# Opening of an encoder kernel: a broadcast weight row, small gate weights, the third unit's weights and the decay sums take other places

## The chip, the cores and the metric

The kernel runs on one core of one Trainium2 chip, as one launch. The metric is the device time of one execution in microseconds (us). Before the change it is 1990.61 us, the median of 3 runs (1989.9 to 1991.65). One further execution was profiled; the profile and its trace are of that one.

The engines are named as the profile names them: PE multiplies matrices (PEld is the loading of its stationary operand), DVE and ACT work on vectors, POOL is the general-purpose engine, SP issues the DMAs. Each engine takes its instructions strictly in the order in which they stand in its own queue. Matrix products go to PSUM, in banks of 128 x 512 numbers; the other tiles lie in SBUF.

## The reference

One layer of an encoder: 1024 tokens and 16 meta tokens of width 1024. The input is normalised, multiplied by one wide matrix `w_in`, and cut into the inputs of two mixers; what matters here is the first one and, in it, the small gates.

```python
h = rmsnorm(h_res, norm1_w[l])
proj = h @ w_in[l]
(q, k, v, z, b_raw, a_raw, sc_b, sc_c, sc_x, gate_a, gate_b) = jnp.split(proj, SPLIT_POINTS, axis=-1)
o_dn = gated_deltanet_bidir(q, k, v, z, b_raw, a_raw, ...)
...
qkv = jax.nn.silu(depthwise_conv_centred(jnp.concatenate([q, k, v], axis=-1), conv_w))
beta = jax.nn.sigmoid(b_raw).reshape(Bsz, L, 2, DN_HEADS)
g = -jnp.exp(A_log) * jax.nn.softplus(a_raw.reshape(Bsz, L, 2, DN_HEADS) + dt_bias)
...
g = jnp.cumsum(g, axis=-1)      # in each chunk of 64 tokens, forwards and backwards
decay = jnp.exp(jnp.where(tri, g[..., :, None] - g[..., None, :], -jnp.inf))
```

The decay `g` is one number for each token, head (8) and direction (2). Its running sums set the decay factors of the scan over chunks that follows. The scan's outputs, a second mixer (a short convolution), a merge, an output projection and a gated feed-forward block make up the rest of the layer.

## The kernel before

Every product of two float32 matrices is made of three PE passes: each operand is split into a high part (the number cast to the type in which PE works, on ACT) and a low part (the difference, on DVE or POOL), and high x high, low x high and high x low are added in one PSUM bank (`dense_steps`, line 331). The normalised, transposed input lies in SBUF as 8 high tiles and 8 low tiles (`hTh`, `al`).

The projection is made of **units** of 128 columns of `w_in`. A unit's weights are fetched by a DMA into one of two raw buffers (`pick`, line 932), split into `wh` and `wl` in four parts (`split_part`, lines 939 and 942: two casts on ACT, two subtractions on DVE), and then 72 matmuls run over the tokens in three chunks. A chunk's bank is copied out by two ACT instructions (lines 387 and 388) when the unit's generator is taken one step past the chunk's last matmul. There are two slots of `wh` and `wl`, and the raw buffer of a unit is free for the next DMA when its low part is made.

The first phase is a hand-ordered **opening** and then a **planned** loop. In the opening nine token tiles of x are loaded (`load`, lines 1008 to 1011), and go through `root` (mean square on ACT, two small POOL instructions for the reciprocal root), `scaled` (one DVE instruction at line 1020 that multiplies a tile by its root and by the row `w1row`, the 1024 norm weights laid on all 128 partitions), `turned` (eight PE transposes, line 83), `highs` (line 1039, ACT) and `lows` (line 1045, DVE). Between them run the first two units (`gen0`, the keys of head 0, and `gen1`, its queries; `steps` takes eight steps, which is one chunk) and the small gates: `small_gates` multiplies the 32 gate columns, whose high and low parts stand in one tile `wba` of 64 columns, with the tokens of a chunk (lines 1051 and 1052). The low half of `wba` is made by DVE at line 1118. `keep_warm` is idle PE work.

After the opening a planner writes the instructions of all engines in one order. It keeps its own clocks `T` of the engines; PE's matmuls are the frame, and jobs (convolutions, gates, decays, inverses, scans) put a piece in when the planner's clock says that its inputs are there. `g_gates` (from line 1192) is the job that turns the small gates into `g` and its sums: transposes of `baT` (line 1205), a chain of small DVE instructions for the logarithm (lines 1212 to 1246), an `affine_select` on POOL that clears the unused rows of the last chunk (line 1250), two copies into the tiles `gc` by direction (line 1255), and for each direction four matmuls with triangular matrices (line 1261) and one more (line 1273). The jobs' pieces stand in the same queues as everything else, so a PE instruction that waits for one of them holds up the units' matmuls behind it.

The lines behind the opening that matter: lines 1298 to 1303 take `gen0` and `gen1` to their ends (which writes the copies of their last chunks), queue `g_gates`, and pick the next two units; the third unit (the values of head 0) is split at the loop's start.

Of the kernel before, what the change touches and what calls it, by code (L numbers as in the profile page):

```python
# [8 lines left out]
F32 = mybir.dt.float32  # L9
# [3 lines left out]
ALU = mybir.AluOpType  # L13
# [3 lines left out]
P = 128  # L17
D = 1024
KT = 8
SEQ = 1024  # L20
META = 16
# [16 lines left out]
def encoder_layer(ctx: ExitStack, tc: tile.TileContext, x, meta, norm1_w, w_in,  # L38
                  dn_conv_w, A_log, dt_bias, dn_norm_w, sc_conv_w, w_bdn, w_bsc,
                  w_out, norm2_w, w_gu, w_down, final_w, out):  # L40
    nc = tc.nc
    x, out = x[0], out[0]
# [22 lines left out]
    def psd():  # L65
        return ps.tile([P, 512], F32, tag="e", name=uid("pe"), bufs=2)
# [29 lines left out]
    def wtiles(shape):  # L96
        return [wp.tile(shape, F32R, tag=g, name=uid(g), bufs=2) for g in ("wh", "wl")]
# [104 lines left out]
    c1 = ph1.enter_context(tc.tile_pool(name="c1", bufs=1))  # L202
# [15 lines left out]
    def on(e, ns, ready=0.0):  # L218

        T[e] = max(T[e], ready, T["pe"]) + ns  # L220
        return T[e] + TOPE
# [766 lines left out]
    with tc.tile_pool(name="st", bufs=1) as st:  # L988
# [17 lines left out]
        def load(t):  # L1006
            if t == 0:
                nc.sync.dma_start(xs[0][:META], meta)
                nc.sync.dma_start(xs[0][META:P], x[0:P - META])
            else:  # L1010
                nc.sync.dma_start(xs[t][:size(t)], x[P * t - META:P * t - META + size(t)])
# [6 lines left out]
        def scaled(t):  # L1018
            p = size(t)
            nc.vector.scalar_tensor_tensor(out=xs[t][:p], in0=xs[t][:p], scalar=rss[t][:p, 1:2], in1=w1row[:p],  # L1020
                                           op0=ALU.mult, op1=ALU.mult)
# [35 lines left out]
        def steps(g, n=KT):  # L1057
            for _ in range(n):
                next(g)
# [5 lines left out]
                transpose(idle[:, :P], ident)  # L1065

        load(0)
        load(1)
        nc.sync.dma_start(w1row, norm1_w[0:1, :].broadcast_to([P, D]))
        load(2)  # L1070
        u0 = pick()
        load(3)
# [41 lines left out]
        nc.scalar.copy(cols[:, :24], pt2[:, :24])  # L1114
        nc.scalar.mul(cols[:, 24:25], pt2[:, 24:25], 0.5)
        nc.scalar.copy(wba[:, :, 0:32], raw_ba)
        scaled(3)
        nc.vector.tensor_tensor(out=wba[:, :, 32:64], in0=raw_ba, in1=wba[:, :, 0:32].bitcast(F32), op=ALU.subtract)
        nc.scalar.copy(u1[1][0], u1[2])
        nc.gpsimd.tensor_tensor(out=u1[1][1], in0=u1[2], in1=u1[1][0].bitcast(F32), op=ALU.subtract)  # L1120
        root(4)
# [36 lines left out]
        lows(8, 0)  # L1158
        lows(8, 1)
        steps(gen0)  # L1160
        steps(gen1)
        small_gates(2)


# [27 lines left out]
    def g_gates():  # L1192
# [4 lines left out]
        nc.sync.dma_start(dtb, dt_bias.rearrange("a b c -> a (b c)").broadcast_to([P, 16]))  # L1197
        nc.sync.dma_start(alg, A_log.rearrange("a b c -> a (b c)").broadcast_to([P, 16]))
        nc.gpsimd.memset(BA, 0.0)
        pba = psd()  # L1200
        pbm = psd()
        for c in range(9):
# [33 lines left out]
        for k in (13, 11, 9, 7, 5, 3, 1):  # L1236
# [6 lines left out]
        nc.vector.tensor_scalar(out=alg, in0=alg, scalar1=-1.0, scalar2=None, op0=ALU.mult)  # L1243
        g = sr
        nc.vector.scalar_tensor_tensor(out=g, in0=a_, scalar=0.0, in1=sr, op0=ALU.max, op1=ALU.add)
        nc.vector.tensor_tensor(out=g, in0=g, in1=alg.unsqueeze(1).broadcast_to([P, 9, 16]), op=ALU.mult)
        nc.vector.tensor_scalar(out=beta, in0=beta, scalar1=0.5, scalar2=0.5, op0=ALU.mult, op1=ALU.add)
        on("dve", 1200)

        nc.gpsimd.affine_select(out=g[:, 8, :], in_=g[:, 8, :], compare_op=ALU.is_gt, fill=0.0,  # L1250
                                base=META, pattern=[[0, 16]], channel_multiplier=-1)
        gcs = [c1.tile([P, 8, 9], F32, name=f"gc{d}") for d in range(2)]
        yield T["dve"] + 700
        for d in range(2):
            nc.vector.tensor_copy(gcs[d].rearrange("p h c -> p c h"), g[:, :, d * 8:d * 8 + 8])
            small_v()
        yield T["dve"] + TOPE
        for d in range(2):
            pt = psd().rearrange("p (a n) -> p a n", a=4)
            for i, m in enumerate((U2[d], U[d], E_[d], ones)):  # L1260
# [34 lines left out]
    for m_ in meta_inv:  # L1295
        nc.gpsimd.memset(m_, 0.0)
    SPL = (4, 6, 8, 10)
    for g in (gen0, gen1):
        for _ in g:
            pass  # L1300
    decs.append([g_gates(), T["pe"], None])
    ahead = [pick(), pick()]
    ahead[0][1] = wtiles([P, KT, P])
    while done < H or qkv_units or fill_units or any(ahead):
        u = ahead.pop(0)
        if u is None:
# [558 lines left out]
```

## Time and profile before

| what | value |
|---|---|
| median of 3 runs | 1990.61 us |
| the profiled execution | 1991.52 us, of which its span (first to last instruction) 1989.5 us |
| mean granted PE clock | 0.994 of full speed |
| DVE, ACT, POOL busy | 1472.7, 868.1, 158.5 us of the span |
| share of the chain that ended last | PE 87%, DVE 8%, ACT 2%, DMA 1% |
| DMA moved | 264.09 MB, mean 133 GB/s |

The span is taken by the profiler on the one core. What lies between the span and the execution's time, 2.0 us, is the start and the end, which no instruction of the kernel fills. A row of the timeline gives an instruction's start, its duration, engine, line and operation, the tiles it writes and reads, how many of its kind follow each other, and in brackets how long its engine sat idle before it and what ended the wait. PE's durations overlap, since matmuls are pipelined; the distance of two starts is what one costs.

### The profile page before, as it was taken

What the parts mean: (1) busy time and instruction counts of PE and PEld (TensorE: products, weight loads), DVE (VectorE), ACT (ScalarE), POOL (GpSimd) and SP (SyncE); (2) the same over time, 40 slices, a digit from 0 to 9 for tenths busy, and PEclk for the clock granted to TensorE, in tenths of its full rate; (3) what the DMA queues carried; (4) which work ended last, traced back from release to release, by engine and by line L of the source; (5) the groups of instructions that cost most, each with busy time, mean ns of one, the idle gap of its engine ahead of it and who ended that gap; (6) DMA issues with size and microseconds to landing.
All of it is one profiled execution on the core that took longest, in us unless ns stands there. A gap on an engine that the chain in (4) does not pass through costs nothing.

```text
span 1989.5 us, 31925 instructions
## 1 busy us (share of the span) xinstructions
PE 1952.8 (98%) x11929; PEld 1709.9 (86%) x11929; DVE 1472.7 (74%) x2799; ACT 868.1 (44%) x2011; POOL 158.5 (8%) x455
## 2 busy tenths in 40 slices
PE   8899999999999999999999999999999999999998
PEld 7898899999999989998888888787888888888887
DVE  4687677888888888787348788559987777856574
ACT  5365435555555555442435545225332322325343
POOL 3002011111111211110000000000000000000001
PEclk9999999999999999999999999999999999999999
DMA  4123323132313131314377533232765445487554
GB/s 143 33 66 112 86 85 97 55 90 65 81 56 89 40 106 56 89 57 160 98 276 251 202 112 120 102 117 95 253 236 194 142 150 179 162 276 246 194 172 167
DMA packets 243279, 264.09 MB, mean 133 GB/s; under 512 B 46836, under 2 KB 166949, under 8 KB 240693
## 3 DMA queue, kind: packets, MB, share of 16 engines
q1 hardware_dynamic: 243125, 262.07, 40.5%
q8 instruction: 93, 1.52, 0.3%
q14 instruction: 61, 0.50, 0.1%
HBM read 189.58 MB, written 72.44 MB: 132 GB/s over the span
## 4 chain that ended last, share of the span: by engine, by line
PE 87%; DVE 8%; ACT 2%; DMA 1%; issue 1%; SPq 0%; POOLq 0%; DVEq 0%; POOL 0%; ACTq 0%
PE pm L331 29%; PE pm L1381 4%; PE pd L1381 4%; PE pm L1646 3%; PE pe L1381 3%; PE pm L1644 3%; PE pm L1645 3%; PE pd L1644 2%; PE pd L1646 2%; PE pd L1645 2%; DVE kq L354 2%; PE pe L1644 2%; PE pe L1646 2%; PE pe L1645 2%; PE pd L813 2%; PE pd L830 1%
## 5 line engine op out<-in xcount | busy, mean ns | idle before, releaser
L331 PE MATMUL pm<-hTh,wh 128*128 128x320 f32 (+4 forms) x1328 | 487.5, 368 | 2.8 <-ACT wh L942 2.8
L331 PE MATMUL pm<-hTh,wl 128*128 128x320 f32 (+4 forms) x1328 | 451.8, 341 | 0.0
L331 PE MATMUL pm<-al,wh 128*128 128x320 f32 (+4 forms) x1328 | 451.1, 341 | 0.5 <-DVE al L1045 0.5
L331 PEld LDWEIGHTS pm<-hTh,wh 128*128 128x128 f32 x1328 | 251.3, 189 | 17.3 <-ACT wh L942 3.1
L331 PEld LDWEIGHTS pm<-hTh,wl 128*128 128x128 f32 x1328 | 250.2, 189 | 15.7 <-DVE wl L939 0.2
L331 PEld LDWEIGHTS pm<-al,wh 128*128 128x128 f32 x1328 | 251.6, 190 | 13.2 <-DVE al L1045 0.7
L87 DVE TENSOR_TENSOR al<-raw,ring_h 128x1024 fp32r<-128x1024 f32 x73 | 88.3, 1223 | 64.6 <-ACT ring_h L86 64.3
L86 ACT CAST ring_h<-raw 128x1024 fp32r<-128x1024 f32 x73 | 76.6, 1053 | 104.4 <-PE pe L1787 36.7
L939 DVE TENSOR_TENSOR wl<-raw,wh 128x512 fp32r<-128x512 f32 x122 | 83.6, 686 | 34.5 <-ACT wh L942 34.3
L354 DVE SCALAR_TENSOR_TENSOR kq<-ra,wc,kq 128x520 f32<-128x520 f32 (+1 forms) x128 | 96.2, 752 | 10.5 <-ACT kq L388 7.8
L128 POOL TENSOR_SCALAR ss<-ss 128x1 f32<-128x1 f32 x12 | 4.1, 343 | 961.9 <-ACT b L1797 606.6
L494 DVE TENSOR_TENSOR fP<-fP,tm 128x135 f32<-128x135 f32 (+23 forms) x248 | 71.7, 289 | 7.2
L490 DVE TENSOR_TENSOR tm<-fP,fN 128x135 f32<-128x135 f32 (+23 forms) x248 | 72.1, 291 | 6.5
L942 ACT CAST wh<-raw 128x512 fp32r<-128x512 f32 x122 | 75.1, 617 | 1.4 <-PE pm L331 1.3
L820 ACT ACTIVATE w<-pd,small 128x128 f32<-128x128 f32 x128 | 40.2, 366 | 78.4 <-PE pd L813 69.6
L842 DVE SCALAR_TENSOR_TENSOR S<-S,eGl,pd 128x128 f32<-128x128 f32 x104 | 31.8, 344 | 54.7 <-PE pd L830 32.6
L87 DVE TENSOR_TENSOR raw<-pair,raw 128x1024 fp32r<-128x1024 f32 (+1 forms) x42 | 48.0, 1144 | 30.3 <-ACT raw L86 30.2
L86 ACT CAST raw<-pair 128x1024 fp32r<-128x1024 f32 (+1 forms) x42 | 41.7, 993 | 57.9 <-PE pd L1381 27.5
L87 DVE TENSOR_TENSOR wl<-pair,wh 128x1024 fp32r<-128x1024 f32 (+1 forms) x42 | 48.1, 1144 | 21.7 <-ACT wh L86 21.5
L1337 DVE TENSOR_TENSOR b<-pd,b 128x512 f32<-128x512 f32 x59 | 39.6, 686 | 30.2 <-PE pd L1646 30.1
L86 ACT CAST wh<-pair 128x1024 fp32r<-128x1024 f32 (+1 forms) x42 | 41.7, 992 | 46.2 <-PE pd L1381 24.9
L1337 DVE TENSOR_TENSOR b<-pm,b 128x512 f32<-128x512 f32 x58 | 39.1, 685 | 22.7 <-PE pm L1646 20.4
(643 smaller groups left out, 4932.8 us busy)
## 6 DMA issues: line engine op xcount, KB each, us to landing
raw<-in_w_in_dram SPq DMA_DIRECT2D x64, 512.0 KB
raw<-in_w_gate_up_dram SPq DMA_DIRECT2D x44, 512.0 KB
sums<-in_w_down_dram SPq DMA_DIRECT2D x22, 512.0 KB
t_d<-sums SPq DMA_DIRECT2D x11, 1024.0 KB
raw<-s_d SPq DMA_DIRECT2D x44, 256.0 KB
raw<-t_d SPq DMA_DIRECT2D x44, 256.0 KB
act_d<-b SPq DMA_DIRECT2D x43, 256.0 KB
raw<-act_d SPq DMA_DIRECT2D x33, 256.0 KB
```

Of the source, the lines that this page charges most:

```text
L86: nc.scalar.copy(hi, src)
L87: nc.vector.tensor_tensor(out=lo, in0=src, in1=hi.bitcast(F32), op=ALU.subtract)
L331: mm(po[:, :n], (wl if j == 2 else wh)[:, k], xl[k][:, t0:t0 + n] if j == 1 else xh[k][:, t0:t0 + n], start=(i == 0), stop=(i == 3 * KT - 1))
L354: nc.vector.scalar_tensor_tensor(out=acc, in0=raw[:, h0 + t:h0 + t + hn], scalar=wc[:, t, col:col + 1], in1=acc, op0=ALU.mult, op1=ALU.add)
L490: nc.vector.tensor_tensor(out=tv, in0=fP[:, 0:r, j:j + 1].broadcast_to([P, r, n]), in1=fN[:, j:j + 1, j + 1:32].broadcast_to([P, r, n]), o ...
L939: nc.vector.tensor_tensor(out=u[1][1][:, k], in0=u[2][:, k], in1=u[1][0][:, k].bitcast(F32), op=ALU.subtract)
L942: nc.scalar.copy(u[1][0][:, k], u[2][:, k])
L1337: add = lambda out, a, b: nc.vector.tensor_tensor(out=out, in0=a, in1=b, op=ALU.add)
L1381: mm(bank[t], a[:, c], b, start=fresh, stop=first and k == 3 and j == 2, skip_group_check=not first)
L1644: mm(po, ah[:, k], bhk, start=k == 0, stop=False)
L1645: mm(po, ah[:, k], blk, start=False, stop=False)
L1646: mm(po, al[:, k], bhk, start=False, stop=k == 3)
```

## The change

Four things are moved or rewritten.

- The DMA of the norm row `w1row` is issued ahead of the second token tile's, not behind it.
- The low half of `wba` is made ahead of `scaled(3)` on DVE, not behind it.
- `gen0` is taken to its end right after its last chunk, and the next two units are picked and the third unit's weights split there, ahead of the last chunk of `gen1` and the last small gates; `gen1` is taken to its end right after its last chunk. Before, all this stood behind the opening.
- In `g_gates` the product with `alg` is written straight into the two `gc` tiles, by direction and apart for the last chunk (four DVE instructions, over only the rows that are used). The tiles are cleared by two memsets on POOL at the job's start. The `affine_select`, the two copies and the planner's pause for them are gone.

```diff
         load(0)
+        nc.sync.dma_start(w1row, norm1_w[0:1, :].broadcast_to([P, D]))
         load(1)
-        nc.sync.dma_start(w1row, norm1_w[0:1, :].broadcast_to([P, D]))
         load(2)
...
         nc.scalar.copy(wba[:, :, 0:32], raw_ba)
+        nc.vector.tensor_tensor(out=wba[:, :, 32:64], in0=raw_ba, in1=wba[:, :, 0:32].bitcast(F32), op=ALU.subtract)
         scaled(3)
-        nc.vector.tensor_tensor(out=wba[:, :, 32:64], in0=raw_ba, in1=wba[:, :, 0:32].bitcast(F32), op=ALU.subtract)
         nc.scalar.copy(u1[1][0], u1[2])
...
         steps(gen0)
+        for _ in gen0:
+            pass
+        ahead = [pick(), pick()]
+        ahead[0][1] = wtiles([P, KT, P])
+        for k in range(4):
+            split_part(ahead[0], k)
         steps(gen1)
+        for _ in gen1:
+            pass
         small_gates(2)
...
         nc.gpsimd.memset(BA, 0.0)
+        gcs = [c1.tile([P, 8, 9], F32, name=f"gc{d}") for d in range(2)]
+        for gc in gcs:
+            nc.gpsimd.memset(gc, 0.0)
...
-        nc.vector.tensor_tensor(out=g, in0=g, in1=alg.unsqueeze(1).broadcast_to([P, 9, 16]), op=ALU.mult)
+        for d in range(2):
+            for c, p in ((slice(0, 8), P), (slice(8, 9), META)):
+                nc.vector.tensor_tensor(out=gcs[d][:p, :, c].rearrange("p h c -> p c h"), in0=g[:p, c, d * 8:d * 8 + 8],
+                                        in1=alg[:p, d * 8:d * 8 + 8].unsqueeze(1).broadcast_to([p, c.stop - c.start, 8]), op=ALU.mult)
         nc.vector.tensor_scalar(out=beta, in0=beta, scalar1=0.5, scalar2=0.5, op0=ALU.mult, op1=ALU.add)
         on("dve", 1200)
-
-        nc.gpsimd.affine_select(out=g[:, 8, :], in_=g[:, 8, :], compare_op=ALU.is_gt, fill=0.0,
-                                base=META, pattern=[[0, 16]], channel_multiplier=-1)
-        gcs = [c1.tile([P, 8, 9], F32, name=f"gc{d}") for d in range(2)]
-        yield T["dve"] + 700
-        for d in range(2):
-            nc.vector.tensor_copy(gcs[d].rearrange("p h c -> p c h"), g[:, :, d * 8:d * 8 + 8])
-            small_v()
-        yield T["dve"] + TOPE
+        yield on("dve", 500) + TOPE
...
-    for g in (gen0, gen1):
-        for _ in g:
-            pass
     decs.append([g_gates(), T["pe"], None])
-    ahead = [pick(), pick()]
-    ahead[0][1] = wtiles([P, KT, P])
```

**In the queues.** The first place is DVE's queue in the opening, around the fourth token tile `xr_158` (line 1020 is `scaled`; `wba_raw` holds the gate columns as loaded). A piece of the difference:

```order
 L1045 TENSOR_TENSOR al_127<-pd_297,hTh_130 128x2x128
 L1045 TENSOR_TENSOR al_128<-pd_297,hTh_130 128x2x128
+L1117 TENSOR_TENSOR wba<-wba_raw,wba 128x8x32
 L1020 SCALAR_TENSOR_TENSOR xr_158<-xr_158,rs_168,w1row 128x1024
-L1118 TENSOR_TENSOR wba<-wba_raw,wba 128x8x32
 L1020 SCALAR_TENSOR_TENSOR xr_159<-xr_159,rs_169,w1row 128x1024
```

The subtraction has gone ahead of one `scaled`.

The second place is ACT's queue at the end of the opening. `pm_585` is the bank of the last chunk of `gen0`, `pm_506` that of the middle chunk of `gen1` and `pm_612` (afterwards `pm_624`) of its last; `pe_637` (afterwards `pe_651`) is the bank of the last small gates; `wh_702` (afterwards `wh_616`) is the third unit's high part. Before:

```order
L387 COPY ra_502<-pm_506 128x320
L388 ACTIVATE kq_318<-pm_506,wc 128x320
L1055 COPY baT<-pe_637 64x384
L387 COPY ra_453<-pm_585 128x384
L388 ACTIVATE kq_318<-pm_585,wc 128x384
L387 COPY ra_502<-pm_612 128x384
L388 ACTIVATE kq_318<-pm_612,wc 128x384
L942 CAST wh_702<-raw_698 128x512 x2
L1208 COPY BA<-pe_722 128x256
```

With the change:

```order
L387 COPY ra_453<-pm_585 128x384
L388 ACTIVATE kq_318<-pm_585,wc 128x384
L942 CAST wh_616<-raw_612 128x512 x2
L387 COPY ra_502<-pm_506 128x320
L388 ACTIVATE kq_318<-pm_506,wc 128x320
L387 COPY ra_502<-pm_624 128x384
L388 ACTIVATE kq_318<-pm_624,wc 128x384
L1055 COPY baT<-pe_651 64x384
L1219 COPY BA<-pe_726 128x256
```

The casts of the third unit's weights stood behind the last small gates' copy and now stand behind the last chunk of `gen0` alone.

The third place is where PE meets the decay sums: `wh_846` (afterwards `wh_850`) is the fifth unit's weight, and the matmuls with `gc` stand between its own. Before:

```order
L331 MATMUL pm_1061<-hTh_130,wl_847 128x384
L1261 MATMUL pe_1085<-gc_1013,U2f 128x72
L1261 MATMUL pe_1085<-gc_1013,Uf 128x72
L1261 MATMUL pe_1085<-gc_1013,Ef 128x72
L1261 MATMUL pe_1085<-gc_1013,ones 128x72
L331 MATMUL pm_1061<-hTh_130,wh_846 128x384
```

With the change:

```order
L331 MATMUL pm_1034<-hTh_129,wl_851 128x320
L1267 MATMUL pe_1049<-gc_722,U2f 128x72
L1267 MATMUL pe_1049<-gc_722,Uf 128x72
L1267 MATMUL pe_1049<-gc_722,Ef 128x72
L1267 MATMUL pe_1049<-gc_722,ones 128x72
L331 MATMUL pm_1034<-hTh_130,wh_850 128x320
```

They stood after 21 matmuls of the unit's third chunk (`pm_1061`, 384 columns) and now stand after 12 of its second (`pm_1034`, 320 columns): 33 matmuls earlier. In the same stretch of DVE's queue the subtraction for the first half of the next unit's weights (line 939), which stood ahead of the end of the decay chain, now stands behind it, and one pair of the chain's instructions has moved ahead of an earlier subtraction of that kind. Since the planner's clocks differ from there on, pieces of the jobs stand at slightly other places on all engines up to about the 990th row of PE's queue (of 9701, with repeated rows merged); from there the order on PE is the same as before.

## The prediction

> **What bounds the kernel.** The page comes first.
>
> ```profile
> span 1989.5 us, 31925 instructions
> PE 1952.8 (98%) x11929; PEld 1709.9 (86%) x11929; DVE 1472.7 (74%) x2799; ACT 868.1 (44%) x2011; POOL 158.5 (8%) x455
> ```
>
> PE is busy for 98% of the span, so time can be won where PE stands idle or runs at a lower clock, and nowhere else. The waits of PE in the first 200 us name the places:
>
> ```profile
> PE pe L1261 <- DVE gc L1255: 2.9, 1, 2.9
> PE pm L331 <- ACT wh L942: 2.8, 1, 2.8
> PE pe L1051 <- DVE wba L1118: 2.7, 1, 2.7
> PE pd L83 <- DVE xr L1020: 2.4, 1, 2.4
> ```
>
> The change goes at all four: 10.8 us of idle PE. The windows show a second price:
>
> ```profile
> 20.00:30.00 10.00, 7.27 (x51) 6.63 (x51) 6.54 (x7) 2.65 (x7) 4.17 (x5) 1.00 0.51 135
> 50.00:60.00 10.00, 7.24 (x40) 5.82 (x38) 0.74 (x2) 3.20 (x7) 0.63 (x3) 0.95 0.00 0
> 60.00:70.00 10.00, 10.00 (x54) 9.49 (x54) 8.32 (x16) 1.60 (x4) 0.00 (x0) 0.71 0.21 57
> 100.00:110.00 10.00, 10.00 (x61) 9.97 (x62) 7.40 (x15) 2.95 (x10) 0.00 (x0) 0.83 0.22 61
> ```
>
> The third number from the end is the granted clock. After the gap of 2.8 us, which lies at 56.5 to 59.3, it is 0.95 and 0.71: 6.8 us at half clock, some 6.6 of them with PE at work, so 3.3 us lost. After the gap of 2.9 at 97 it is 0.83: 3.4 us at half, 1.7 lost. After the gap of 2.7 at 20 it stays full.
>
> **The norm row.**
>
> ```profile
> 5.96 1.06 ACT L1015 ACTIVATE jk_first<-xr 128x1024 f32<-128x1024 f32 x1 [3.68 <-DMA xr<-in_x_dram]
> 7.14 1.06 ACT L1015 ACTIVATE jk_first<-xr 128x1024 f32<-128x1024 f32 x1
> 8.69 0.58 POOL L130 TENSOR_TENSOR rs<-rs,minus_half 128x1 f32<-128x1 f32 x1
> 8.95 2.48 DVE L1020 SCALAR_TENSOR_TENSOR xr<-xr,rs,w1row 128x1024 f32<-128x1024 f32 x2 [8.95 <-DMA w1row<-in_norm_w_dram]
> 10.32 1.06 ACT L1015 ACTIVATE jk_first<-xr 128x1024 f32<-128x1024 f32 x1 [2.02 <-DMA xr<-in_x_dram]
> ```
>
> Four transfers of 512 KB land in the order of their issue: the first tile by 5.9 us, the second by 7.1, the row by 8.9, the third tile by 10.3. With the row second it lands near 7.1, and the first `scaled` starts when its root is there (8.1), 0.8 earlier. But the second tile then lands near 8.9 and not 7.1; its root follows 2.1 us later (7.14 to 9.27 in these rows), at 11.0, and its `scaled` starts at 11.0 instead of 10.2. It holds up the third's, which stands behind it on DVE, by some 0.3. The first unit starts when the third tile is through. I take **+0.25 us**; the ends are -0.5 (the second tile lands no later) and +0.4.
>
> **The small gates' low part.**
>
> ```profile
> 17.81 0.41 ACT L1116 CAST wba<-wba_raw 128x256 fp32r<-128x256 f32 x1
> 19.05 1.28 DVE L1020 SCALAR_TENSOR_TENSOR xr<-xr,rs,w1row 128x1024 f32<-128x1024 f32 x1 [1.58 <-POOL rs L130]
> 19.25 3.28 POOL L1120 TENSOR_TENSOR wl<-raw,wh 128x1024 fp32r<-128x1024 f32 x1 [0.23 <-ACT wh L1119]
> 20.25 2.56 DVE L1118 TENSOR_TENSOR wba<-wba_raw,wba 128x256 fp32r<-128x256 f32 x1
> 64.13 0.42 DVE L1212 TENSOR_TENSOR BA<-pe,BA 128x256 f32<-128x256 f32 x1
> ```
>
> The subtraction of 256 elements takes 2.56 us, though another of that size takes 0.42, and it ends at 22.8, 0.3 us behind POOL's subtraction: it was held by POOL. Its input is ready at 18.2, and DVE idles for 1.58 us just then. Ahead of `scaled(3)` it runs in that idle time and ends by about 18.7, or by 19.4 if POOL's small root instructions hold it; PE, which waited 2.7 us for it, then finds it done. **-2.7 us** (to -2.0). `scaled(3)` may start 0.4 later; PE needs it only after the small gates' 16 matmuls, so that is hidden, and costs 0.4 at most without them.
>
> [...]
>
> **The third unit's weights.**
>
> ```profile
> 56.18 0.34 PE L1051 MATMUL pe<-hTh,wba 128*64 128x384 f32 x1
> 56.55 0.47 ACT L1055 COPY baT<-pe 64x384 f32<-64x384 f32 x1 [9.82 <-PE pe L1051]
> 59.26 1.29 DVE L939 TENSOR_TENSOR wl<-raw,wh 128x512 fp32r<-128x512 f32 x2 [13.71 <-ACT wh L942]
> 59.28 0.65 PE L331 MATMUL pm<-hTh,wh 128*128 128x336 f32 x1 [2.76 <-ACT wh L942]
> ```
>
> ACT idles for 9.8 us ahead of 56.5 and DVE for 13.7 us ahead of 59.3. Two casts (0.6 each, as the one at 85.03 below) and the subtractions (1.29) move into that time. They stand behind the end of `gen0`'s last chunk, near 49.4 (24 matmuls of 384 columns at 0.173, worked out below, and the small gates' 16 lie between it and 56.2), behind two bank copies and are done near 52.5. PE then starts the unit at 56.35 and not 59.28: 2.93. After three matmuls stand the transposes of `baT`, which ACT copies until 57.02; that is a new wait of some 0.3, with the unit's other matmuls queued behind it. So -2.6, and with the gap the half clock goes: -3.3. PE would be **5.9 us** ahead. The copies of `pm_506` that now stand behind the casts end near 52, ahead of the third unit, which takes that bank. The next unit's DMA, which waits for the subtractions, goes out near 52.5 instead of 60.55 (59.26 + 1.29), and the two small ones behind it on SP too.
>
> **What is late next: the decay sums.**
>
> ```profile
> 61.79 0.37 ACT L1208 COPY BA<-pe 128x256 f32<-128x256 f32 x1 [2.04 <-PE pe L83]
> 66.03 0.31 DVE L1215 TENSOR_TENSOR a__764<-BA,dtb 128x144 f32<-128x144 f32 x1 [1.40 <-DMA dtb<-in_dt_bias_dram]
> 63.70 0.64 ACT L359 ACTIVATE rb<-kq 128x520 f32<-128x520 f32 x1 [0.95 <-DVE kq L354]
> 67.48 3.14 DVE L354 SCALAR_TENSOR_TENSOR kq<-ra,wc,kq 128x520 f32<-128x520 f32 x4
> 85.03 0.62 ACT L942 CAST wh<-raw 128x512 fp32r<-128x512 f32 x1
> 92.69 0.31 DVE L1246 TENSOR_TENSOR sr<-sr,alg 128x144 f32<-128x144 f32 x1
> 99.50 0.33 DVE L1255 COPY gc<-sr 128x72 f32<-128x72 f32 x2
> 99.87 0.61 PE L1261 MATMUL pe<-gc,U2f 128*128 128x72 f32 x2 [2.91 <-DVE gc L1255]
> ```
>
> The product with `alg` stands at 92.7, the copies at 99.5: between them DVE works at a convolution and weights. The change writes `gc` at the first place. From 59.3 to 99.5 DVE is nearly never idle, so I follow it. The nine transposes end near 57.8 by estimate, ACT's copies at 58.4; five DVE instructions of 0.2 to 0.4 take it to 59.75 (the bias has landed, no 1.40 of wait), a weight half to 60.35, one convolution step to 61.1, ACT's tanh (0.64) to 61.85, its product to 62.5: the four steps of the row at 67.48 start at 62.5, 5.0 earlier. From there to the product it was 25.2 us; 0.6 falls away (a weight half that now stands behind) and 0.5 (one pair of the chain now fills the wait for the cast at 85.03). So 86.6, and the four products in place of one: two for the first direction, where two copies took 0.33 and one product 0.31, so 0.3 to 0.6, say 0.4: `gc` stands at **87.0**, PE starts 12.9 us earlier than at 99.87. The memsets on POOL lie in its idle time.
>
> But PE arrives earlier as well. The matmuls of the sums stand 33 ahead of where they stood: 12 of 320 columns and 21 of 384.
>
> ```profile
> 89.64 0.30 PE L331 MATMUL pm<-hTh,wh 128*128 128x320 f32 x1
> 93.15 0.34 PE L331 MATMUL pm<-hTh,wh 128*128 128x384 f32 x1
> 96.62 0.34 PE L331 MATMUL pm<-hTh,wl 128*128 128x384 f32 x1
> ```
>
> 24 starts in 3.51 us are 0.146 each, 20 in 3.47 are 0.173: 5.4 us of work moves behind the sums. PE would be there at 85.45 (91.4 for the twelfth matmul, less 5.9) and waits until 87.0: a wait of 1.55 in place of 2.91. Net, the same work is done 12.9 - 5.4 = **7.5 us** earlier (by PE's own account 5.9 + 1.4 = 7.3; I take 7.4). The 1.7 us of half clock behind it go if the shorter wait doesn't bring it on again; gaps of 2.8 and 2.9 did, one of 2.7 did not, and I keep 0.6 of it: **-1.1** (-1.7 to +1.6, the loss after the other gap).
>
> [...]
>
> **Behind 100 us.** PE's lead lasts if DVE keeps up.
>
> ```profile
> 104.29 0.29 DVE L1276 COPY rr<-pe 72x128 f32<-72x128 f32 x1 [1.43 <-PE pe L1273]
> 143.39 0.67 PE L582 MATMUL pe<-kq 128*128 128x256 f32 x2 [0.20 <-DVE PQ L616]
> 143.84 0.59 DVE L612 SCALAR_TENSOR_TENSOR NP<-pe,small,PQ 128x128 f32<-128x128 f32 x2
> 145.03 0.41 DVE L616 TENSOR_TENSOR PQ<-pe,PQ 128x256 f32<-128x256 f32 x1
> 145.99 0.59 PE L582 MATMUL pe<-kq 128*128 128x256 f32 x2
> ```
>
> DVE's lead of 5.0 grows where it waited for PE (1.43 in this row, and once more behind it), to about 7; PE's is 8.5. They meet at line 582, where PE waited 0.2: I charge **+0.5** (0 to 3, since the order there is mixed anew).
>
> **Sum:** 0.25 - 2.7 - 7.4 - 1.1 + 0.5 = -10.45 us. Against the profiled 1991.52 that is 1981.1; the 2.0 us outside the span stay. The median is 0.9 lower, and the forecast for it is **1980.2**. Ends: all small ones low, -0.5 - 2.7 - 8.1 (`gc` 0.7 earlier) - 1.7 = -13.0, 1977.6; all high, 0.4 - 2.0 - 6.7 + 1.6 + 3 = -3.7, 1986.9.
>
> **Rivals.** *DVE keeps the gate.* If the chain gains only half of 5.0 (a bank copy or the tanh is late), `gc` stands near 89.5, PE waits 4, and half clock returns: 2.5 + 1.7 less, 1984.4. For it: DVE is the fuller engine from 59 to 99. Against: each step of the walk has its row.
>
> *The subtraction of `wba` is still held by POOL*, because the cast on ACT comes later: 2.7 less, 1982.9. Against: POOL's long one starts only after another cast that stands behind on ACT.
>
> *The shorter wait brings no half clock:* 0.6 more, 1979.6. The window at 20 us speaks for it, those at 50 to 70 against. [...]
>
> *Slower: line 582.* PE's rows there wait two chunks back for line 616. Per chunk DVE spends 0.59 + 0.41 and one convolution step of 0.77 (a quarter of the row at 67.48), 1.8 in all; PE comes by after 2.6 us (143.39 to 145.99). If the mixed order lets PE come 0.95 too early at each of 16 chunks of two heads, 15 us go: 1995. It beats the gain from 0.65 per chunk. Against: one wait of 0.2 there before.
>
> **How the numbers follow.** Forecast 66%, DVE's gate 16%, `wba` 6%, no half clock 6%, line 582 6% (two thirds of it slower than before). About 0.2%, or 4.0 us, is what a measurement can tell from no change. Forecast, `wba` and the clock's case are faster; of DVE's gate 11 in 16; of line 582 none: 0.89 faster, 0.07 same, 0.04 slower. The range from 1977.5 to 1985.8 holds the forecast but for 8%, and most of the gate's case.
>
> **What would show it.** No PE wait at lines 1051 and 331 ahead of 60 us; the clock full from 56 to 66; the unit's start at 53.9 (56.35 less 2.45); the sums' first matmul near 84.5, after a wait of 1 to 2 us; `wba` in 0.4 us. Wrong: half clock behind the sums for over 4 us, waits at line 582 over 3 us in all, or a wait at line 331 for weights.

## The result, and the profile after

| kernel | executions | median us | lowest to highest | ratio to before |
|---|---|---|---|---|
| before | 6 | 1991.13 | 1989.90 to 1997.73 | |
| changed | 6 | 1984.00 | 1981.65 to 1985.09 | 0.9957, 95% interval 0.9944 to 0.9970 |

The changed kernel is faster by 0.43% (0.30 to 0.56), some 8.6 us of 1991 (6.0 to 11.1). That is by the ratio, which is not formed from the two medians; these are 7.1 us apart. The forecast was 1980.2, and a gain of 10.45 us; the time is 3.8 us above it, inside the range, and the forecast gain lies inside the interval of the measured one. The profiled execution of after took 1984.74 us, its span 1982.5, which is 7.0 below the span of before.

PE's waits in the first 130 us of the changed kernel, from the view of waits (in all, times, longest):

```profile
PE pd L83 <- DVE xr L1020: 2.9, 3, 1.8
...
PE pe L1267 <- DVE gc L1259: 1.2, 1, 1.2
PE pe L83 <- ACT hTh L1039: 0.8, 1, 0.8
...
PE pe L83 <- DVE Nm L565: 0.5, 1, 0.5
...
PE pe L1267 <- ACT eGl L1275: 0.3, 1, 0.3
```

The waits of 2.7 at L1051 and of 2.8 at L331 are gone, and that for the decay sums fell from 2.9 to 1.2. The wait of the norm row is now in three pieces. The timeline of the changed kernel shows the steps of the forecast (code lines are a few higher than before):

```profile
17.89 0.43 DVE L1117 TENSOR_TENSOR wba<-wba_raw,wba 128x256 fp32r<-128x256 f32 x1 [0.55 <-ACT wba L1116]
...
20.16 0.32 PE L1051 MATMUL pe<-hTh,wba 128*64 128x336 f32 x1
...
53.44 0.34 PE L1051 MATMUL pe<-hTh,wba 128*64 128x384 f32 x1
53.62 0.31 PE L331 MATMUL pm<-hTh,wh 128*128 128x336 f32 x1
...
83.90 0.51 DVE L1259 TENSOR_TENSOR gc<-sr,alg 128x64 f32<-128x64 f32 x4
...
84.34 0.41 PE L1267 MATMUL pe<-gc,U2f 128*128 128x72 f32 x2 [1.24 <-DVE gc L1259]
```

Before, the first small-gate matmul stood at:

```profile
22.86 0.36 PE L1051 MATMUL pe<-hTh,wba 128*64 128x336 f32 x1 [2.73 <-DVE wba L1118]
```

The small gates' subtraction took 0.43 us and not 2.56. PE came to the first small-gate matmul at 20.13 before (22.86 - 2.73) and comes to it at 20.16 now, and no longer waits there. The third unit follows the small gates at once, at 53.62 (forecast 53.9), with matmuls 0.15 us apart, and the granted clock from 50 to 60 us is 1.00. The sums start at 84.34 (forecast 84.55) after 1.24 us of wait (forecast 1.55).

A good mark for what the opening as a whole is worth is the first small matmul of L705, since from there on PE's order is the same in both. The view of one line gives durations, then the first and last start. Before:

```profile
L705 PE MATMUL pd<-XT,NP x256: 191/191/212, 226.8 to 908.4; 32*32 32x32 f32 x128
```

After:

```profile
L705 PE MATMUL pd<-XT,NP x256: 191/191/212, 215.9 to 898.5; 32*32 32x32 f32 x128
```

PE is 10.9 us ahead at the first and 9.9 at the last, while the span is 7.0 shorter. So in this pair of executions the opening gave what the forecast's sum said, and 3.9 us went later. The timeline of after shows where:

```profile
808.59 0.42 PE L331 MATMUL pm<-hTh,wl 128*128 128x320 f32 x1 [1.04 <-issue]
...
903.85 0.21 PE L713 MATMUL pd<-NP,T 32*32 32x32 f32 x1 [2.02 <-issue]
...
1353.66 0.79 PE L1647 MATMUL pm<-b_hl,wl 128*128 128x512 f32 x1 [2.75 <-DVE wl L87]
...
1778.92 0.50 PE L1786 MATMUL pm<-ring_h 128*128 128x512 f32 x1 [1.41 <-ACT ring_h L86]
```

And that of before, at the same matmuls (the first has no wait there):

```profile
912.59 0.18 PE L713 MATMUL pd<-NP,T 32*32 32x32 f32 x1 [0.93 <-issue]
...
1362.49 0.50 PE L1646 MATMUL pm<-b_hl,wl 128*128 128x512 f32 x1 [2.75 <-DVE wl L87]
...
1785.89 0.50 PE L1785 MATMUL pm<-ring_h 128*128 128x512 f32 x1 [0.79 <-ACT ring_h L86]
```

Two waits that no semaphore explains ("issue") cost 1.04, and 2.02 - 0.93 = 1.09. Between the last two rows the lead falls from 1362.49 - 1353.66 = 8.83 to 1785.89 - 1778.92 = 6.97: 0.62 for the longer wait at `ring_h`, and 1.24 behind a wait of 2.75 us that is the same in both. That one is the clock. Windows of before (PE's busy time first, the granted clock third from the end):

```profile
1359.46:1362.87 3.41, 0.67 (x4) 0.33 (x3) 3.41 (x6) 3.38 (x4) 0.00 (x0) 1.00 0.00 0
1362.87:1366.29 3.42, 3.42 (x10) 2.65 (x9) 3.42 (x5) 0.69 (x2) 0.00 (x0) 0.50 0.00 0
1366.29:1369.70 3.41, 3.41 (x17) 2.80 (x16) 3.17 (x5) 1.21 (x2) 0.00 (x0) 1.00 0.80 293
```

Of after:

```profile
1349.51:1352.92 3.41, 1.40 (x9) 0.89 (x7) 3.41 (x5) 3.02 (x5) 0.00 (x0) 1.00 0.00 0
1352.92:1356.33 3.41, 2.67 (x6) 2.15 (x7) 3.41 (x4) 1.80 (x3) 0.00 (x0) 0.50 0.00 0
1356.33:1359.74 3.41, 3.41 (x9) 2.64 (x8) 3.41 (x5) 0.59 (x1) 0.00 (x0) 0.50 0.43 154
1359.74:1363.16 3.42, 3.42 (x16) 2.80 (x15) 1.93 (x4) 1.62 (x3) 0.00 (x0) 1.00 0.41 158
```

In both traces the clock changes only at the edges of a grid of 3.41 us (within 3 ns of it), on which these windows are laid. Before, the wait lies in one stretch (0.67 us busy) and one stretch of half clock follows. After, it lies across an edge, and two follow.

### The profile page after: what moved, and what is told of

The parts are those of the page before. It is cut to its first block, busy times and chain, and to the rows that moved or that the text cites. A ratio compares the mean times of both kernels' runs of the same rounds, so it can differ in the third digit from the quotient of the medians.

```text
span 1982.5 us, 31924 instructions
## 1 busy us (share of the span) xinstructions
PE 1948.7 (98%) x11929; PEld 1705.1 (86%) x11929; DVE 1471.9 (74%) x2800; ACT 868.1 (44%) x2011; POOL 158.3 (8%) x456
## 4 chain that ended last, share of the span: by engine, by line
PE 89%; DVE 7%; ACT 1%; issue 1%; DMA 1%; SPq 0%; POOL 0%; POOLq 0%; DVEq 0%; ACTq 0%
PE pm L331 31%; PE pm L1382 4%; PE pd L1382 4%; PE pm L1647 3%; PE pm L1646 3%; PE pm L1645 3%; PE pe L1382 3%; PE pd L1646 3%; PE pd L1645 3%; PE pd L1647 3%; PE pe L1646 2%; PE pe L1645 2%; PE pe L1647 2%; DVE kq L354 2%; PE pd L813 2%; PE pd L830 1%
## 5 line engine op out<-in xcount | busy, mean ns | idle before, releaser
L331 PE MATMUL pm<-hTh,wh 128*128 128x320 f32 (+4 forms) x1328 | 486.0, 367 | 0.1
L331 PE MATMUL pm<-hTh,wl 128*128 128x320 f32 (+4 forms) x1328 | 450.6, 340 | 1.0 <-issue 1.0
L331 PE MATMUL pm<-al,wh 128*128 128x320 f32 (+4 forms) x1328 | 449.8, 340 | 0.5 <-DVE al L1045 0.5
L331 PEld LDWEIGHTS pm<-hTh,wl 128*128 128x128 f32 x1328 | 249.1, 188 | 16.8 <-issue 1.3
L331 PEld LDWEIGHTS pm<-hTh,wh 128*128 128x128 f32 x1328 | 250.2, 189 | 14.3 <-ACT kq L388 0.3
L331 PEld LDWEIGHTS pm<-al,wh 128*128 128x128 f32 x1328 | 250.5, 189 | 13.2 <-DVE al L1045 0.7
```

The lines of the kernel that those rows point to most:

```text
L331: mm(po[:, :n], (wl if j == 2 else wh)[:, k], xl[k][:, t0:t0 + n] if j == 1 else xh[k][:, t0:t0 + n], start=(i == 0), stop=(i == 3 * KT - 1))
```

## The experiments

The theory to test: the parts do what the forecast says; what was lost behind them belongs to single executions (where the grid lies, when code is fetched, which of two engines comes first) and not to the change. The rival: it belongs to the changed program.

The runs were made in four batches, each with the kernel before beside it: the two kernels again and the two parts (median of before 1992.53 us, 23 executions); the small gates, the row's place and the late wait (1994.23, 15); the 64 small matmuls and the first of the two put together (1993.18, 15); the 32 small matmuls and the second put together (1993.42, 9). Ratios are to the kernel before of the same batch, so across batches they say more than the times do.

**Both kernels again, unaltered.**

> The changed kernel once more, unaltered. In its first trace PE is 10.9 us ahead of the kernel before at the first small matmul of line 705 (215.91 against 226.80), as the forecast's sum had it, and 7.0 at the end; the 3.9 go in four places: issue waits of 1.04 at L331 (808.6) and of 2.02 against 0.93 at L713 (903.9), half clock of 6.83 in place of 3.41 behind L1647 (1353 to 1360), and 1.41 against 0.79 at L1786. Theory: these belong to one execution and not to the change; the lead at L705 comes again within 0.4, while at least one of the issue waits differs from its first value by 0.5 or more, or the half clock behind L1647 is 3.41. Rival: they belong to the program, and all come again at the same place within 0.2 us.

> The kernel before once more, unaltered, for one profile. Theory: the clock is granted in stretches of 3.41 us, and which of its waits brings half clock depends on how the wait lies to their edges; a stretch with about 2.0 us or more of idle PE is followed by half clock, so the sums' wait of 2.9 and the wait of 2.7 at L1646 bring it again, and the wait of 2.7 at L1051 (1.30 and 1.43 us on the two sides of an edge the first time) brings none if the edges lie as before. The first small matmul of L705 stands within 1.7 us of 226.8. Rival: the half clock is bound to the place in the program, with exactly 3.4, 6.8, 3.4, 3.4 and 3.4 us at the same five places.

The changed kernel: 1983.97 us (1981.04 to 1986.22, 6 executions), ratio 0.9953 (0.9937 to 0.9969). The kernel before: 1988.93 for the profiled one. In the new trace of after:

```profile
902.73 0.21 PE L713 MATMUL pd<-NP,T 32*32 32x32 f32 x1 [1.64 <-issue]
```

```profile
900.54:903.95 3.41, 1.77 (x77) 1.49 (x68) 0.78 (x2) 0.83 (x3) 0.00 (x0) 1.00 0.24 90
903.95:907.36 3.41, 3.41 (x9) 2.66 (x9) 2.38 (x4) 1.73 (x4) 0.00 (x0) 0.50 0.26 96
...
1354.51:1357.92 3.41, 3.38 (x8) 2.71 (x9) 3.41 (x5) 1.10 (x2) 0.00 (x0) 0.50 0.00 0
1357.92:1361.33 3.41, 3.41 (x16) 2.80 (x16) 3.19 (x5) 1.05 (x2) 0.00 (x0) 1.00 0.65 196
```

L705 starts at 216.6, so the lead came again within 0.7 and not, as expected, within 0.4. The wait at L331 near 810 is gone, that at L713 is 1.64, half clock behind L1647 lasts one stretch and not two, and `ring_h` is waited for 0.48 instead of 1.41; but L713's wait has brought a stretch of half clock of its own. All four losses changed in the same program: the rival, by which all come again at the same size, falls.

In the new trace of before L705 starts at 223.3, not 226.8. The expectation (within 1.7 us) was missed by 1.8, and the reason is instructive. PE's idle time at the first tiles was spread over two stretches of the grid (1.15 and 1.24 us) and brought no half clock. In the first trace of before 2.42 us of it lay in one stretch, and one of half clock followed (first two rows; the other two are the small gates' wait, which lay across an edge):

```profile
7.78:11.20 3.42, 1.00 (x9) 0.91 (x9) 2.25 (x2) 1.40 (x3) 1.10 (x3) 1.00 1.08 356
11.20:14.61 3.41, 3.41 (x18) 3.41 (x17) 2.87 (x6) 2.38 (x7) 0.79 (x2) 0.50 1.07 328
...
18.02:21.44 3.42, 2.12 (x14) 1.83 (x12) 2.39 (x2) 2.20 (x4) 3.02 (x4) 1.00 1.07 353
21.44:24.85 3.41, 1.99 (x13) 1.57 (x14) 2.63 (x2) 0.00 (x0) 1.94 (x3) 1.00 0.78 192
```

The rival of this run, half clock at the same five places in every execution, falls at this one of the five; at the other four it came again. At the small gates the second trace has:

```profile
18.20 0.42 DVE L1118 TENSOR_TENSOR wba<-wba_raw,wba 128x256 fp32r<-128x256 f32 x1
18.30 2.57 POOL L1120 TENSOR_TENSOR wl<-raw,wh 128x1024 fp32r<-128x1024 f32 x1 [1.34 <-ACT wh L1119]
```

DVE came 0.10 us ahead of POOL and was not held; PE did not wait at L1051 at all. So the opening of before is itself 3.5 us better or worse by chance, and the change is worth 226.8 - 215.9 = 10.9 us against the one execution and 223.3 - 216.6 = 6.7 between the two others. The second execution is the rarer one: of the 68 executions of before in all batches one is shorter than its 1988.93.

From the first matmul of L705 to the end of the span the two traces of before take 1762.7 and 1763.6 us, those of the changed kernel 1766.6 and 1764.7. The run with the small gates alone (below), which has the order of before there, takes 1764.5. With so few traces it is not ruled out that 1 to 2 us of the loss belong to the change.

**Two parts alone.** Only the third unit's weights (the hunks at `ahead` and `gen0`, `gen1`), and only the decay sums (the hunks on `gcs`):

```diff
+        ahead = [pick(), pick()]
+        ahead[0][1] = wtiles([P, KT, P])
+        for k in range(4):
+            split_part(ahead[0], k)
         steps(gen1)
```

```diff
-            nc.vector.tensor_copy(gcs[d].rearrange("p h c -> p c h"), g[:, :, d * 8:d * 8 + 8])
+                nc.vector.tensor_tensor(out=gcs[d][:p, :, c].rearrange("p h c -> p c h"), in0=g[:p, c, d * 8:d * 8 + 8],
```

> Of the change only the third unit's weights. Theory: its first matmul stands at about 56.4 instead of 59.28 and the half clock of 6.8 us around it goes, so PE is 5.9 us ahead; the copies of the decay sums then come only 5.0 earlier, PE waits about 3.8 for them, and the first small matmul of L705 stands at about 221.8 (lead 5.0), or 223.5 if the longer wait brings two stretches of half clock. Time 5 us less than before (3.3 to 6). Rival: the copies stay where they were, the wait swallows the lead, and under 1.5 us remain.

> Of the change only the decay sums written straight into the matmuls' tiles. Theory: the products stand at about 93.2 and PE, which comes there at 91.4 with 33 matmuls (5.4 us) now behind the sums, waits 1.8 us: 1.3 us of lead, and 1.7 more if that wait brings no half clock. L705 at about 223.8 (225.5 with half clock), time 3.0 us less (1.0 to 3.2). Rival: the same matmuls are only moved behind the sums and nothing is gained: L705 at 226.6 or later.

Measured: 0.9983 (0.9970 to 0.9996), 3.4 us (0.8 to 6.0), for the unit; 0.9982 (0.9973 to 0.9991), 3.6 us (1.8 to 5.4), for the sums. The unit alone, at the sums (its line numbers):

```profile
95.29 0.46 PE L1269 MATMUL pe<-gc,U2f 128*128 128x72 f32 x1 [3.69 <-DVE gc L1263]
```

```profile
91.68:95.09 3.41, 0.00 (x0) 0.00 (x0) 2.10 (x5) 2.64 (x6) 0.10 (x1) 1.00 0.00 0
95.09:98.50 3.41, 3.21 (x13) 3.24 (x14) 2.73 (x7) 0.47 (x3) 0.00 (x0) 0.50 0.56 154
98.50:101.92 3.42, 3.42 (x16) 3.38 (x14) 0.76 (x2) 1.49 (x3) 0.00 (x0) 0.50 0.04 10
```

The longer wait that was expected (3.8) came, as 3.69, and with it two stretches of half clock. L705 stands at 224.9 (expected 221.8, or 223.5 with that half clock): 1.9 ahead of the first trace of before, 1.6 behind the second. This execution, the longest of its twelve (1996.35), had a stretch of half clock at 23.4 us, and its last small-gate matmul stood at 57.05, 0.87 behind before. The time, 3.4 us less, is at the low end of what was expected (3.3 to 6); its interval does not shut out the rival (under 1.5). The sums alone:

```profile
93.58 0.30 PE L1259 MATMUL pe<-gc,U2f 128*128 128x72 f32 x1 [1.06 <-DVE gc L1251]
```

A wait of 1.06 and no half clock behind it; L705 again at 224.9, 1.9 ahead of the first trace of before (expected 3.0): two smaller waits behind the sums (0.54 for `eGl`, 0.83 for `Nm`) took a part back, as they do in the changed kernel (0.26 and 0.49). The time is 3.6 us less, above the 1.0 to 3.2 that were expected, and the rival (nothing gained) falls. In the traces the first part moves PE's wait to the sums and the second shortens it. The times show no coupling of the two: 3.4 and 3.6 us, and 2.4 for the small gates below, add up to 9.4, the gain of the whole in the first batch (0.9953).

**The small gates alone, and the row's place undone.**

```diff
+        nc.vector.tensor_tensor(out=wba[:, :, 32:64], in0=raw_ba, in1=wba[:, :, 0:32].bitcast(F32), op=ALU.subtract)
         scaled(3)
```

```diff
-        nc.sync.dma_start(w1row, norm1_w[0:1, :].broadcast_to([P, D]))
         load(1)
+        nc.sync.dma_start(w1row, norm1_w[0:1, :].broadcast_to([P, D]))
```

> Of the change only the small gates' low part ahead of the fourth tile. The forecast gave it 2.7 us. In the second trace of the kernel before, the same subtraction took 0.42 us where it stood: DVE began it at 18.20, 0.1 ahead of POOL's subtraction, and PE did not wait at L1051; in three other traces with that order PE waited 2.73, 1.83 and 1.91 there. Theory: in this kernel PE never waits at L1051 and the subtraction takes 0.42 to 1.0, so the time is 1.3 to 2.4 us less than the median of before (an average over executions that are held and ones that aren't), not 2.7. Rival: 2.7 us in all executions.

> The changed kernel with w1row's load third again, as before. The forecast had the row's place at +0.25 us for the change. Theory: the time is that of the changed kernel within 0.6 us (0.25 less), PE's first matmuls on the tiles wait about 2.4 us in one piece in place of two or three pieces, and whether that brings half clock for 3.41 us (1.7 lost) depends on where the edges of the 3.41 us stretches lie. Rival: the new place splits the wait and so always saves the half clock; then this kernel is 1.5 us slower than the changed one.

The small gates alone: 0.9988 (0.9978 to 0.9998), 2.4 us with 0.4 and 4.4 as ends. In the trace the subtraction runs ahead of `scaled(3)`, and PE has no wait at L1051:

```profile
17.86 0.42 DVE L1117 TENSOR_TENSOR wba<-wba_raw,wba 128x256 fp32r<-128x256 f32 x1 [0.98 <-ACT wba L1116]
```

The interval takes in 2.7 too, so the time alone decides nothing between theory and rival; the trace of before that was not held does. Without the row's new place: 1982.61 us (1981.64 to 1983.65, 4 executions), ratio 0.9940 (0.9924 to 0.9955), not slower than the changed kernel's 1984.00 and 1983.97. The rival (1.5 slower) falls, and the time is 1.4 less, outside the 0.6 of the theory. L705 stands at 215.3 here and at 215.1 in the last run below, which lacks the new place too, against 215.6 to 216.6 in four traces that have it. So the row's new place gains nothing that can be seen, and may cost 0.3 to 1.5.

**The late wait: kept warm, or shortened.** First 20 transposes of the identity into the bank that the next product overwrites; then the third pair's weights split ahead of the last norm tile's work on DVE:

```diff
         po = psany()
+        for _ in range(warm):
+            transpose(po[:, :P], ident)
```

```diff
+    third = stationary1(2)
     norm_T(*late_norm)
...
-    ahead.append(part1(stationary1(2), *p1_2))
+    ahead.append(part1(third, *p1_2))
```

> The changed kernel with 20 transposes of the identity into the bank ahead of the third pair of the gate's products, so that PE works through most of the wait of 2.75 us at L1647; nothing else is altered, and the matmul that waits can start no earlier. Theory: a stretch of 3.41 us with about 1.9 us or more of idle PE brings half clock in the next; with 0.6 us of idle time left it stays full, and the time is 1.7 us less than the changed kernel's (3.4 in executions where the wait lay across an edge). Rival: the half clock there has another cause than idle time; it comes all the same, and the time is the changed kernel's.

> The changed kernel with the third pair's weights split ahead of the last norm tile's work on DVE, so that the subtraction for which L1647 waits stands ahead of three subtractions of 0.6 us. Theory: the wait falls from 2.75 to about 0.9 us and the half clock behind it goes: 1.8 and 1.7 us, 3.5 less than the changed kernel (1.8 to 5.2). Rival: what stood ahead is now behind, and the next matmuls (on T2 or S2) wait for it: the time is the changed kernel's within 1 us.

Kept warm: executions of 1978.29, 1978.91 and 1983.47 us (a fourth took 5011.86 and is not in the ratio); ratio 0.9927 (0.9909 to 0.9945). At the wait:

```profile
1356.34 0.50 PE L1647 MATMUL pm<-b_hl,wl 128*128 128x512 f32 x1 [0.55 <-DVE wl L87]
```

```profile
1352.90:1356.30 3.40, 2.89 (x22) 2.36 (x20) 3.40 (x6) 3.37 (x5) 0.00 (x0) 1.00 0.00 0
1356.30:1359.70 3.40, 3.36 (x15) 2.77 (x16) 3.40 (x5) 1.70 (x3) 0.00 (x0) 1.00 0.02 5
```

The clock stays full (1.00 in both rows) with 0.51 us of idle time in the stretch, where 2.01 and 2.72 brought half clock in the two traces of the changed kernel: idle time is the cause of the half clock there. The median of the three is 5.1 us below the changed kernel, more than the 1.7 to 3.4 expected, but three executions of another batch don't price it. The longest of the three is the profiled one; half clock came there behind L713 and for two stretches at L1587. In each of the fourteen traces the clock's edges lie within 3 ns of a grid of 3.41 us, and the grid starts at another place in each. A stretch that was only partly idle brought half clock: 2.0 us of 3.41 were enough, as the windows of after at 1349.51 show.

Split ahead: 1983.60 (1981.60 to 1986.84, 4 executions), no gain. The waits of its trace from 1340 to 1400 us:

```profile
PE pe L1647 <- DVE s_hl L87: 1.1, 1, 1.1
PE pm L1647 <- DVE wl L87: 0.9, 1, 0.9
PE pe L1645 <- ACT s_hl L86: 0.8, 1, 0.8
PE pd L1646 <- DVE b L87: 0.3, 1, 0.3
```

The wait fell to 0.9 as computed, and 2.2 us of new waits stand behind it, with a stretch of half clock at 1372. The rival was right: DVE is busy for 13.31 of 13.64 us in four stretches of the grid between 1348 and 1376, and here the order only chose who waits.

**Waits without a semaphore.** The view of DMA lists the transfers by queue; q8 carries instructions. For the whole changed kernel, and then for 1.15 us of it from 901.35 (transfers, MB, share of the engines):

```profile
q8 instruction: 93, 1.52, 0.3%
...
q8 instruction: 1, 0.02, 5.5%
```

The 93 transfers of 16 KB go with PE's 11929 matmuls and as many loads of weights: one for some 257 instructions. None lies in the 3.35 us ahead of 901.35, while the data took 102.5% of the engines' time. PE stopped at 901.83, and went on at 903.85. To move the code against its 16 KB blocks:

```diff
             pt = psd().rearrange("p (a n) -> p a n", a=4)
+            for _ in range(0 if d else 64):
+                mm(pt[:32, 0, :32], ident[:32, :32], ident[:32, :32], start=True, stop=True)
```

> The changed kernel with 64 matmuls of 32x32 into the bank of the first decay sums, ahead of them: about 1.0 us of work inside PE's wait of 1.24 us there, and 128 instructions that move all later ones of PE by 128 places against the 16 KB blocks in which they are fetched; nothing else is altered. In eight traces with one order of PE's instructions from 200 us on, PE waited 0.93 to 2.05 us at L713 near 905 us, with no semaphore to wait for, and in four of them 1.04 to 1.60 at L331 near 810. Theory: PE has run out of instructions there. A fetch starts when the last block is begun; it falls into the first of two bursts of small matmuls and is late behind transfers of 512 KB, and the second burst uses up what is left. Moved by 128 places, the fetches fall ahead of the first burst and into the second, so both waits go (under 0.3 us), and the time is 1.5 us less than the changed kernel's (0.5 to 3). Rival: the waits come from the transfers or the banks alone; then 0.9 to 2.0 us stay at L713.

Measured 1986.39 us (1984.54 to 1987.94, 10 executions), 2.4 more than the changed kernel (by the ratio, 0.9962, 1.0 to 1.8 more, with intervals that overlap). The wait at L713 stayed, at 1.91. The sums' row showed why:

```profile
83.05 4.23 PE L1267 MATMUL pe<-ident 32*32 32x32 f32 x128
```

64 written matmuls are 128 passes, each with a load of weights: 256 instructions, a whole block by the 257 above, so the fetches had kept their places, and 4.23 us stood in place of a wait of 1.24. With half as many (`range(0 if d else 32)`):

> As the run with 64 small matmuls, with 32 of them. A written matmul of this type is two on PE, as the trace of that run shows (128 of them in 4.23 us), so that run moved the code by 256 places, a whole block of 16 KB, and left the fetches where they were; this one moves it by 128. Theory: in twelve traces the wait at L713 stands before the 81st or 82nd matmul of the burst, and ends 2.4 us after the start of the fetch that falls into the two bursts; with the fetches half a block earlier it goes (under 0.3 us at L713), and so does any wait at L331 near 810. The 64 passes take 2.1 us in place of a wait of 1.24, and may bring half clock for 3.4 us: the time is the changed kernel's within 1.5 us. Rival: 0.9 to 2.0 us stay at L713, and the wait has nothing to do with the blocks.

Measured 1983.62 (1981.63 to 1984.03, 4 executions), the changed kernel's time. At the place of the wait, and the waits from 390 to 920 us:

```profile
902.63 0.21 PE L713 MATMUL pd<-NP,T 32*32 32x32 f32 x1
```

```profile
PE pd L713 <- issue: 0.5, 1, 0.5
PE pd L715 <- issue: 0.9, 1, 0.9
```

It is gone at 902 and at 810, as expected; 0.89 and 0.54 us of the same kind have come at two earlier bursts (408.9 and 608.4). So in these two runs the wait at L713 goes with the fetches of PE's code: moved by 256 places it stayed at 1.91, moved by 128 it went; one trace shows the move. That data transfers make a fetch late is argued from the DMA rows and was not tried by itself. The 257 instructions per transfer of 16 KB and the two moves agree with each other.

**Put together.** The changed kernel without the row's new place, kept warm at L1647, with 22 transposes ahead of L1585 (written as those above), and with or without the 64 small matmuls:

> The changed kernel with w1row's load third again, the 64 small matmuls ahead of the decay sums, the 20 transposes ahead of the third pair's products, and 22 transposes into the first bank of the output product ahead of L1585, which waits 0.75 and, four matmuls on, 2.06 us. Theory: the waits themselves stay about as long as they are in sum, but no stretch of 3.41 us has 1.6 us of idle PE between 20 and 1970 us, so the clock stays full there: 1.7 us each at L1587 and L1647, 1.5 from the two waits without semaphore; 5 us less than the changed kernel, about 1979 (1977 to 1981). Rival: the first bank is read until late, so that the 22 transposes start late and hold up L1585: 2 us are lost again, about 1981.

> The combined kernel without the small matmuls: the changed kernel with w1row's load third again, the 20 transposes ahead of the third pair's products and the 22 ahead of L1585. In the combined run the small matmuls took 4.23 us in place of a wait of 1.24 and brought half clock for 3.41, and that run measured 1982.1. Theory: without them 3.0 and 1.7 us are saved: 1977.5 (1976 to 1979.5), with full clock from 20 to 1970 us in executions where the wait at L713 does not bring half clock. Rival: the small matmuls had also shortened the waits behind them, and under 2 us are saved.

With them 1982.11 (1980.59 to 1985.69, 6 executions), ratio 0.9943 (0.9925 to 0.9962), 3 above the expected 1979 and outside its range: they cost about what they had cost before. Without them 1979.61 (1977.16 to 1980.98, 5 executions), ratio 0.9926 (0.9911 to 0.9941), 2.5 less (expected 4.7), just outside the range of 1976 to 1979.5. Its highest time lies below the lowest of the changed kernel's twelve (1981.04): it beats both kernels, though the kernel before was no faster in this batch. What each of its parts gives is not told apart. The wait at L1587 kept its 2.0 us and its stretch of half clock; the 22 transposes filled only the waits of 0.53 and 0.75 ahead of it.

## Why the prediction was right, and where it was not

- **Norm row, +0.25.** PE came to the small gates at 20.13 before and at 20.16 after. Right in size, but with luck: the forecast took no account of the half clock at 11.20 that the row's wait of 2.42 us had brought in the profile of before, and none came in this profile of after; in the second one it came, at 13.07. Over all traces the new place looks a little worse than forecast (0.3 to 1.5).
- **Small gates, -2.7.** The last small-gate matmul stands at 53.44 against 56.18, 2.74 earlier for this and the row (forecast 2.45). Right against the profiled execution, where the subtraction took 2.56 us and ended 0.28 behind POOL's (20.25 + 2.56 against 19.25 + 3.28), against 0.42 us with the change. Wrong as a price for all: in the four traces with the old order PE waited 2.73, 1.83, 1.91 and 0 us there.
- **Third unit, -2.6 and -3.3.** Start at 53.62 against 59.28, 5.66 (forecast 5.38), and full clock behind it (1.00). Right; the new wait of 0.3 at the transposes of `baT`, which the forecast had counted, did not come.
- **The gate, -7.4.** 99.87 - 84.34 = 15.5, less the 5.4 of matmuls moved behind, 10.1; the forecast had 2.45 + 7.4 = 9.9 (the third unit's 5.9 is in the 7.4). Right; the trace of the unit alone, where PE waits 3.69 us at the sums, shows that its lead is of use only as far as the sums come earlier too.
- **Clock behind the sums, -1.1.** No half clock came after the 1.24 us, so all of the 1.7 was won, 0.6 more than was counted.
- **Behind 100 us, +0.5.** Waits of 0.26 (`eGl`) and 0.49 (`Nm`); no wait of size at L582. Right in size, but not at the place that was named.
- **The sum.** Lead at L705 10.9 us in the profiled pair, forecast 10.45: the mechanism held. The weakest step is the last: "Against the profiled 1991.52 that is 1981.1", and 0.9 less for the median. It took the profiled execution of before and three further ones as the rule, and all that lay behind 150 us as fixed. Neither holds. The 1990.61 was a low draw: of the 68 executions of before in all batches 56 are longer than the profiled 1991.52, and their median is 1993.30. In the first batch, where both kernels ran again, before takes 1992.53 and the changed kernel 1983.97. So of the 3.8 us between forecast and time 1.9 are the start, which was that much too low, and 1.9 are the gain, 8.56 by these medians in place of 10.45; by the ratio it is 9.4 (6.2 to 12.5), and the forecast gain is inside. What took the 1.9 from the gain stays open. The traces show two things that can: the small gates' wait and the half clock at the first tiles don't come in every execution of before (10.9 us of lead in one pair of traces, 6.7 in another), and each execution draws its own losses behind the opening (3.9 us in the profiled pair).

The rival on the clock ("the shorter wait brings no half clock") is what happened at the sums; the others did not come.

## What to carry to other kernels

Before a wait is priced from one profile, ask whether it repeats, and whether the time it is taken from is a usual one: here PE waited 2.73 us where DVE's subtraction began 1.0 us behind POOL's and not at all where it began 0.1 ahead, and of two gaps of 2.7 us in one trace the one across an edge of the clock's grid (1.30 and 1.43 us on its sides) brought no half clock and the one inside a stretch brought 3.41 us of it, so look at a second trace of the same kernel. Where a wait of 2.75 us could not be removed, 20 transposes into a bank that is overwritten anyway kept the clock at 1.00 here, and reordering DVE, busy for 13.31 of 13.64 us, gave nothing. A wait that is taken away can come back at the input that is late next, as the 3.69 us at the sums did with the third unit's weights alone, so that one is to be brought earlier too.

## What the runs showed of the hardware

- **The clock's grid.** Laid on the grid of 3.41 us, the fourteen traces have (from the starts and ends of PE's matmuls, from 5 to 1960 us, stretches at full clock) 33 stretches with 1.95 us or more of idle PE: all are followed by half clock. Of 7907 with under 1.6 us three are, and those three hold the 32x32 matmuls of the sums' bank; at 1.6 to 1.95 us seven of eleven are. This answers why, in the forecast, gaps of 2.8 and 2.9 us brought half clock and one of 2.7 did not: that one lay across an edge, with 1.30 and 1.43 us on its sides (the rows of 18.02 to 24.85 above).
- **Half clock behind a stretch full of small matmuls.** In the run with 64 of them the profile has PE never idle, and half clock came, as in the two other traces with such a stretch:

```profile
84.10:87.50 3.40, 3.40 (x104) 3.36 (x101) 3.26 (x10) 0.00 (x0) 0.00 (x0) 1.00 0.03 5
87.50:90.92 3.42, 3.42 (x16) 3.42 (x16) 2.07 (x3) 1.89 (x4) 0.10 (x1) 0.50 0.00 0
```

- **Waits by the fetches of PE's code.** That PE has run out of code there is read from the fetches and the run that moved them; why a fetch is late is open. At the three such waits over 0.9 us of the first two traces PE had done 527 (before, 911.66), 541 and 533 (after, 807.54 and 901.83) matmuls and loads since the fetch before the last one started (at 886.66, 784.51 and 876.47), some two blocks of 257. In thirteen traces the wait at L713 stands before the 81st or 82nd matmul of one burst and ends 2.2 to 2.7 us after the start of the fetch that falls there; it lasted 0.93 to 2.05 us.
